# Moving one weight's pre-additions from the closing stage into the second half of a Winograd-form trunk kernel, regrouping the others, and deferring the gates' sigmoids

## The chip, the cores and the metric

The kernel runs on one core of one Trainium2 chip. The metric is device time in microseconds (us) of one execution. The engines go by these names: TensorE (PE, with PEld for its weight loads), VectorE (DVE), ScalarE (ACT), GpSimd (POOL), SyncE (SP), whose queue (SPq) issues nearly all DMAs.

## The reference, cut to what matters

The input x has 2048 rows of 1024 columns. All of it is fp32.

```python
shift, scale, gate = split(silu(c) @ w_ada + b_ada)
u = x * (1 + scale) + shift
q, k, v, a_gate, p_in, p_gate, m_a, m_p = split(u @ w_in)
a = (sliding_window_sink_attention(q, k, v, ...) * silu(a_gate)) @ w_attn_proj
p = ((multiscale_causal_pool(p_in) mixed per group) * pool_scale * silu(p_gate)) @ w_pool_proj
y = sigmoid(m_a) * a + sigmoid(m_p) * p
y = (y @ w_out) * (1 + gate)
out = layer_norm(alpha * x + y)
```

## The kernel before, in words

**The multiplications.** Every large product is done by the Winograd form of Strassen's scheme: the two operands are cut into 2x2 blocks, and seven block products replace eight. A `Quad` is one such multiplication for two output tiles. Its weight side is loaded into tiles `W` and `A` (lines 253 to 266). GpSimd makes the weight sums `sum1`, `mid` and `late` (lines 268 to 278), four of 128x512 per quad, two of them in `mid`. The other side is a *set*: seven tiles named B11, T1, T2, B21, T3, B22 and T4, of which the T's are sums of raw blocks (T1 = B12 - B11, T2 = B22 - T1, T4 = B21 - T2, T3 = B22 - B12; the code makes them in place). To keep fp32 accuracy each operand is split in a high part (a cast on ACT, line 306) and a low part (a subtraction on DVE, line 132), and one block product is three passes of four multiplications of 128x128 by 128x512. These twelve multiplications are called a product below; the code calls `tick` after each.

**The rings.** `ring` runs groups of two quads: ten products in `back`, four in `front`, so fourteen ticks for a group. `hooks[(group, tick)]` holds functions that are traced at that tick, and `defer(n, f)` traces `f` n ticks on. Instructions of `pe`, `act`, `dve`, `pool`, `sp` stay in the order in which they are traced; those of `nc.scalar` and so on may be moved by the scheduler. Each engine then executes its own instructions in that order, and an instruction that waits holds what is behind it.

**The stages.** A first half (its rings of gates, then attention), a second half (the same: its rings run from about 605 to 828 us, then attention to about 1178 us), and the closing stage ("mix"): a group that ends the second half, two groups of the attention projection and two of the pool projection for the first half of the rows, the same four for the second half, and four groups of w_out with the layer norm. The groups of the closing stage are numbered 0 to 12 here, with ticks counted through: group 1 is ticks 14 to 27. The set changes between two phases: its seven tiles are loaded and split in the last group of one phase and the first five ticks of the next (`planned`, `SPLIT_AT`), so from group 0 into 1, 2 into 3, 4 into 5, 6 into 7 and 8 into 9.

**The sums.** A set's raw blocks lie in DRAM, and before the set can be loaded its four T's must be there too. `sums_to` makes them for one of four slices: it loads two 128x1024 rooms (`spare`) by four DMAs of 256 KB, subtracts four times on POOL (128x512 each), and puts the four results by four DMAs of 256 KB. In the second half's rings it does so for the first half's `ain_d[0]` and `pin_d[0]`; for w_out it loads the weight, multiplies by 1 + gate on DVE and puts the four raw blocks, without sums. The closing stage then makes the sums of `ain_d[1]`, `pin_d[1]` and `wo_d`, one slice every eight ticks from tick 2 to tick 90 (line 1572). In the second half the starts are the tuple of line 1493, where 14 is the first tick of the second ring. `ph.spare()` takes rooms in turn from a cycle that includes the tiles of q, k and v until `ph.turns.clear()` is called, and four rooms of its own after that.

**The gates.** `gates_ahead` (line 599) loads the merge gates of a quad from DRAM and applies the sigmoid (line 607) right behind the load; the consumers are lines 618, 627 and 629 on DVE.

Of the kernel before, what the change touches and what calls it, by code (L numbers as in the profile page):

```python
# [14 lines left out]
AF = mybir.ActivationFunctionType  # L15
# [45 lines left out]
def kernel(  # L61
# [22 lines left out]
    nc = tc.nc  # L84
# [30 lines left out]
    def set_store(name):  # L115
        return {n: dp.tile([2, P, 2, CH], F32, name=f"{name}_{n}") for n in set_names}

    u1_d = set_store("u1")
    wo_d = set_store("wo")
    ain_d = [set_store(f"ain{s}") for s in range(2)]  # L120
    pin_d = [set_store(f"pin{s}") for s in range(2)]
# [3 lines left out]
    def cols(t, n):  # L125
        return t[:, n * CH : (n + 1) * CH]
# [69 lines left out]
    def put(q, store, name, i, src):  # L196
        q.dma_start(store[name][i // 2, :, i % 2, :], src)

    def sums_to(ph, store, i, load, work=None, sums=True):

        b = []

        def x(r, c):
            return b[r][:, c * CH : (c + 1) * CH]

        def fetch():
            b.extend((ph.spare(), ph.spare()))
            b.reverse()
            for r in (1, 0):
                load(b[r], r)  # L210

        def sub(out, a, c):
            return lambda: pool.tensor_tensor(x(*out), x(*a), x(*c), ALU.subtract)

        todo = [(0, fetch)]
        if work:
            todo += [(3, lambda: work(b[0], 0)), (3.5, lambda: work(b[1], 1))]
        made = [("B11", (0, 0)), ("B21", (1, 0)), ("B22", (1, 1))] if work else []
        if work and not sums:
            made.insert(1, ("B12", (0, 1)))  # L220
        puts = [(5 + 0.6 * n, *x) for n, x in enumerate(made)]
        if sums:
            at = 7.5 if work else 4
            for out, a, c, name in (
                ((0, 1), (0, 1), (0, 0), "T1"),
                ((1, 1), (1, 1), (0, 1), "T2"),
                ((1, 0), (1, 0), (1, 1), "T4"),
                ((0, 0), (1, 1), (0, 0), "T3"),
            ):
                todo.append((at, sub(out, a, c)))  # L230
                puts.append((at + 2.5, name, out))
                at += 1.5
        for at, name, z in puts:
            todo.append((at, lambda name=name, z=z: put(sp, store, name, i, x(*z))))
        return sorted(todo, key=lambda t: t[0])
# [9 lines left out]
    class Quad:  # L245
# [7 lines left out]
        def load(self, ph, own, q=nc.sync, e=nc.gpsimd):  # L253
            self.w, self.a22 = ph.weights(), ph.last(own)
            x = self.w
            if len(self.srcs[0].shape) == 3:
                for dst, src, half in ((x[:, 2, :], 1, 0), (self.a22, 1, 1), (x[:, 0, :], 0, 0), (x[:, 3, :], 0, 1)):
                    q.dma_start(dst.rearrange("p (k q) -> p k q", k=4), self.srcs[src][:, 4 * half : 4 * half + 4, :])
                if e is not None:
                    self.sum1(e)  # L260
                return
            q.dma_start(x[:, 2, :], self.srcs[1][:, 0:CH])
            q.dma_start(self.a22, self.srcs[1][:, CH:])
            q.dma_start(x[:, 0::3, :], by_two(self.srcs[0]))
            if e is not None:
                self.sum1(e)
# [187 lines left out]
    def defer(ticks, f):  # L454
        due.append((now[0] + ticks, len(due), f))
# [140 lines left out]
    def wide(ph, i):  # L596
        return ph.t.tile([P, D], F32, tag=f"wide{i}", bufs=1, name=f"wide{i}")

    def gates_ahead(name, s, m, raw):
        g = {}  # L600

        def ahead(ph, turn):
            for mi, t in (((0, 0), (1, 1)), ((0, 1), (1, 0)))[turn]:
                x = g[mi, t] = ph.c("g")
                sp.dma_start(x, gates_d[name][s, m + mi, t])
                if raw:
                    nc.scalar.activation(x, x, AF.Sigmoid)

        return g, ahead

# [854 lines left out]
    def second_phase(ph, opened, post, plan1):  # L1465
        groups, fills, _, turn = plan1
        cb = ph.t.tile([P, D], F32, tag="cb", bufs=1, name="cb")
        hooks = {}

        def gate_rows():  # L1470
            nc.scalar.dma_start(gate_d.rearrange("k p -> p k"), mod[:, 16:24], allow_slow_non_contiguous=True)
            nc.scalar.dma_start(cb, gate_d.rearrange("k p -> (k p)").partition_broadcast(P))

        def load_wo(x, k):
            for n in range(2):
                sp.dma_start(cols(x, n), wout[k, n])

        side = []
        for raw in (ain_d[0], pin_d[0]):
            for i in range(4):  # L1480
                side.append(sums_to(ph, raw, i, load_raw(raw, i)))
        for i in range(4):
            ks = (i, 4 + i)
            side.append(sums_to(
                ph,
                wo_d,
                i,
                lambda x, r, ks=ks: load_wo(x, ks[r]),
                lambda x, r: dve.tensor_tensor(x, x, cb, ALU.mult),
                False,  # L1490
            ))
        ahead, hooks = hooks, {}
        for start, todo in zip((14, 18.5, 23, 27.5, 32, 36.5, 41, 45.5, 57, 61, 65, 69), side):
            for offset, f in todo:
                at = int(start + offset) - 14
                hooks.setdefault((at // 14, at % 14), []).append(f)
        later_hooks, hooks = hooks, ahead
        hooks.setdefault((0, 2), []).append(gate_rows)
        planned(hooks, ph, u1_d, True)
        opened = ring(ph, [post], opened, hooks, groups[0], lambda tick: [front(ph, q, tick) for q in groups[0]])  # L1500
        hooks = later_hooks
        planned(hooks, ph, None, False)
        hooks.setdefault((3, 0), []).append(lambda: ph.turns.clear())
        turned(hooks, lambda i: turn(ph, i), 4)
        opened_by = [q for _, _, q in fills[:2]]
        return ring(ph, groups, opened, hooks, opened_by, lambda tick: [front(ph, opened_by[0], tick)])
# [54 lines left out]
    with Pools("mix", spare=4, p=2, c=8) as ph:  # L1561
        for k in range(4, KT):
            ta[k] = wide(ph, k)
        phases = [([plans[1][2]], None)]
        for s in range(2):
            phases.append((pairs(lambda m, s=s: attn_quad(s, m)), ain_d[s]))
            phases.append((pairs(lambda m, s=s: pool_quad(s, m)), pin_d[s]))
        outs = [out_quad(k) for k in range(0, S // P, 2)]
        phases.append(([outs[i : i + 2] for i in range(0, 8, 2)], wo_d))
        every = [(i, gi) for i, (groups, _) in enumerate(phases) for gi in range(len(groups))]  # L1570
        sides = [{} for _ in phases]
        for n, (raw, i) in enumerate((raw, i) for raw in (ain_d[1], pin_d[1], wo_d) for i in range(4)):
            for offset, f in sums_to(ph, raw, i, load_raw(raw, i)):
                at = int(2 + 8 * n + offset)
                i, gi = every[at // 14]
                sides[i].setdefault((gi, at % 14), []).append(f)
        for i, (groups, store) in enumerate(phases):
            hooks = sides[i]
            if i:
                planned(hooks, ph, store, False)  # L1580
            after, nxt = None, []
            if i + 1 < len(phases):
                planned(hooks, ph, phases[i + 1][1], True, groups=groups)
                nxt = phases[i + 1][0][0]
                after = lambda tick, nxt=nxt: [front(ph, q, tick) for q in nxt]
            else:
                for at, row in ((1, 2), (1, 3), (5, 4), (5, 5)):
                    hooks.setdefault((0, at), []).append(lambda row=row: load_z(ph, row))
            if i in (3, 5):
                ta.clear()  # L1590
            if i == 4:

                def vectors():
                    for name, src in (("gain", gain), ("lnb", lnb)):
                        vec[name] = wide(ph, len(vec))
                        sp.dma_start(vec[name], src.partition_broadcast(P))

                hooks.setdefault((-1, 5), []).append(vectors)
                hooks.setdefault((-1, 7), []).append(lambda: [load_z(ph, row) for row in range(2)])
            opened = ring(ph, groups, opened, hooks, nxt, after, i == 5)  # L1600
# [53 lines left out]
```

## Time and profile before

| what | value |
|---|---|
| median of 3 runs | 1692.15 us (1687.09 to 1692.64) |
| the profiled execution's own time | 1693.3 us |
| its span, first to last instruction | 1691.5 us |
| mean granted TensorE clock | 0.994 |
| PE busy | 1648.7 us, 97% of the span |
| DVE, ACT, POOL busy | 1193.7, 1030.0, 988.5 us |
| mean DMA rate | 199 GB/s |

The profile comes from one execution, whose own time is 1.8 us above its span and 1.15 us above the median of the runs. A row of the view by stretches gives, for a window in us from the start of the span, the busy time of each engine with its number of instructions, the granted clock, the share of the 16 DMA engines in use and the rate. A row of a timeline gives start, duration, engine, line, operation and tiles; brackets at its end hold the idle time before it and who ended that. A row of a group of instructions has the count, the busy time and the mean duration in ns, then the idle time before them.

### The profile page before, as it was taken

Reading aid. Unit: us, or ns where it says so; the run is one execution under the profiler, and the core shown is the slowest. Engines: PE = TensorE matmul, PEld = TensorE weight load, DVE = VectorE, ACT = ScalarE, POOL = GpSimd, SP = SyncE. Lnnn points to the kernel's source line nnn. Section 1 sums busy time; section 2 is a strip of 40 time slices with the busy share of each in tenths; the row PEclk is TensorE's granted clock in tenths of the full one; section 3 lists DMA queues with packets and bytes.
Section 4 is the critical chain, followed back from the end, with each engine's and each line's share of the span. In section 5 each row is a group of like instructions: output and inputs, shape, how many; then the busy total and the mean of one; then the engine's idle time right before and its main releaser. Section 6 shows DMA issues by size and latency. Waiting matters only on the chain.

```text
span 1691.5 us, 24675 instructions
## 1 busy us (share of the span) xinstructions
PE 1648.7 (97%) x8058; PEld 1384.4 (82%) x8058; DVE 1193.7 (71%) x2132; ACT 1030.0 (61%) x2150; POOL 988.5 (58%) x734
## 2 busy tenths in 40 slices
PE   7999999999999999999999999999999999999997
PEld 6788888888888888888788888888878777887886
DVE  6856545676857657357567677676669897989877
ACT  4755457878778755335578777876646445644452
POOL 3343437586857828762476867496567576533442
PEclk9999999999999999999999999999999999999999
DMA  9688843343432478766533344234979797888443
GB/s 359 219 279 307 197 161 102 101 132 108 149 107 99 135 248 308 267 231 211 190 114 99 114 130 156 81 114 135 336 247 363 262 360 259 318 283 271 150 150 112
DMA packets 188849, 336.79 MB, mean 199 GB/s; under 512 B 18336, under 2 KB 44080, under 8 KB 188720
## 3 DMA queue, kind: packets, MB, share of 16 engines
q1 hardware_dynamic: 185600, 330.96, 57.3%
q10 hardware_dynamic: 3088, 4.23, 1.0%
q8 instruction: 64, 1.05, 0.2%
q14 instruction: 65, 0.53, 0.1%
q0 software_dynamic: 32, 0.02, 0.0%
HBM read 227.96 MB, written 110.33 MB: 200 GB/s over the span
## 4 chain that ended last, share of the span: by engine, by line
PE 74%; DVE 8%; DMA 7%; ACT 4%; issue 3%; POOL 3%; SPq 1%; POOLq 0%; DVEq 0%; ACTq 0%
PE mm L57 48%; PE lg L57 19%; PE pv L57 4%; PE pt L57 4%; DVE w_set L132 1%; DMA ain_T<-spare 1%; ACT L L57 1%; DMA g<-ma_d 1%; DMA g<-mp_d 1%; DVE w_set L57 1%; DVE set_T L57 1%; POOL W L269 1%; DMA spare<-pin_B 1%; DVE L L57 1%; ACT w_set L57 1%
## 5 line engine op out<-in xcount | busy, mean ns | idle before, releaser
L57 PE MATMUL mm<-set_B,w_set 128*128 128x512 f32 x2664 | 655.8, 393 | 2.2 <-DVE w_set L132 1.2
L57 PEld LDWEIGHTS mm<-set_B,w_set 128*128 128x128 f32 x2664 | 497.1, 189 | 107.0 <-DVE w_set L132 2.4
L57 PE MATMUL mm<-set_T,w_set 128*128 128x512 f32 x1824 | 455.5, 396 | 5.9 <-DVE mm L57 3.9
L57 PE MATMUL lg<-set_T,w_set 128*128 128x512 f32 x1704 | 412.6, 392 | 10.5 <-DVE p L390 4.4
L57 PEld LDWEIGHTS mm<-set_T,w_set 128*128 128x128 f32 x1824 | 336.7, 189 | 76.2 <-DVE mm L57 6.5
L57 PEld LDWEIGHTS lg<-set_T,w_set 128*128 128x128 f32 x1704 | 319.9, 189 | 81.8 <-ACT w_set L306 5.2
L132 DVE TENSOR_TENSOR w_set<-W,w_set 128x1024 fp32r<-128x1024 f32 x137 | 197.8, 1445 | 142.3 <-ACT w_set L306 129.3
L306 ACT CAST w_set<-W 128x1024 fp32r<-128x1024 f32 x137 | 143.8, 1050 | 212.7 <-PE mm L57 124.3
L57 POOL TENSOR_TENSOR w_set<-W,w_set 128x512 fp32r<-128x512 f32 x120 | 157.3, 1318 | 116.9 <-ACT w_set L57 112.0
L269 POOL TENSOR_TENSOR W<-W,A 128x512 f32<-128x512 f32 x46 | 74.1, 1610 | 232.5 <-DMA A<-in_win_dram 63.5
L57 DVE TENSOR_TENSOR o<-pv,o 64x128 f32<-64x128 f32 x256 | 72.1, 282 | 133.7 <-ACT o L57 127.3
L57 POOL TENSOR_TENSOR spare<-spare 128x512 f32<-128x512 f32 x68 | 124.0, 1826 | 31.5 <-DMA spare<-pin_B 12.2
L57 POOL TENSOR_TENSOR W<-W 128x512 f32<-128x512 f32 x82 | 108.3, 1336 | 53.2 <-DVE sm L57 31.0
L57 ACT ACTIVATE L<-L,nm 128x257 f32<-128x257 f32 (+1 forms) x256 | 127.2, 499 | 9.3 <-DVE nm L57 3.7
L278 POOL TENSOR_TENSOR W<-W 128x512 f32<-128x512 f32 x46 | 72.8, 1583 | 95.9 <-DVE w_set L132 83.5
L57 DVE CUSTOM_DVE_ANT_0 L<-lg,bt,nsink 128x256 f32<-128x256 f32 (+1 forms) x256 | 111.7, 473 | 21.3 <-PE lg L57 11.9
L57 ACT CAST w_set<-W 128x512 fp32r<-128x512 f32 (+1 forms) x165 | 101.4, 628 | 20.9 <-POOL W L57 14.9
L273 POOL TENSOR_TENSOR W<-W 128x512 f32<-128x512 f32 x44 | 72.7, 1656 | 66.3 <-DVE w_set L132 57.2
L57 ACT COPY o<-pv 64x256 f32<-64x256 f32 x128 | 47.4, 370 | 75.9 <-PE pv L57 74.7
L57 DVE TENSOR_TENSOR ptl<-pt,pth 128x512 fp32r<-128x512 f32 (+1 forms) x128 | 85.7, 669 | 1.3 <-ACT pth L57 1.0
L274 POOL TENSOR_TENSOR W<-W 128x512 f32<-128x512 f32 x44 | 71.6, 1628 | 21.9 <-DMA W<-in_win_dram 18.9
L57 ACT ACTIVATE L<-L,sm 128x256 f32<-128x256 f32 (+1 forms) x128 | 64.3, 502 | 31.7 <-DVE sm L57 31.4
(230 smaller groups left out, 2398.2 us busy)
## 6 DMA issues: line engine op xcount, KB each, us to landing
W<-in_win_dram SPq DMA_DIRECT2D x42, 512.0 KB, 5.4
W<-in_win_dram SPq DMA_DIRECT2D x42, 256.0 KB, 3.7
A<-in_win_dram SPq DMA_DIRECT2D x42, 256.0 KB, 4.9
ag_d<-sig SPq DMA_DIRECT2D x32, 256.0 KB, 5.7
pg_d<-sig SPq DMA_DIRECT2D x32, 256.0 KB, 4.4
pg<-pg_d SPq DMA_DIRECT2D x32, 256.0 KB, 3.2
pin_B<-fin SPq DMA_DIRECT2D x32, 256.0 KB, 2.0
ag<-ag_d SPq DMA_DIRECT2D x32, 256.0 KB, 2.9
```

The lines of the kernel that those rows point to most:

```text
L57: return lambda *args, **kw: self.tc.keep_in_program_order(op(*args, **kw))
L132: engine.tensor_tensor(dst, src, as32(hi), ALU.subtract)
L269: e.tensor_tensor(self.w[:, 1, :], self.w[:, 2, :], self.a22, ALU.add)
L273: e.tensor_tensor(x[:, 1, :], x[:, 1, :], x[:, 0, :], ALU.subtract)
L274: e.tensor_tensor(x[:, 2, :], x[:, 0, :], x[:, 2, :], ALU.subtract)
L278: e.tensor_tensor(x[:, 3, :], x[:, 3, :], x[:, 1, :], ALU.subtract)
L306: a.copy(by_two(hi), raw)
```

## The change

It does three things. The four T sums of w_out are made in the second half's rings, right behind the scaling, so w_out's B12 isn't stored any more, and the closing stage makes no sums for w_out; the starts in the second half move together to make room, and `ph.turns.clear()` comes one group earlier. In the closing stage the remaining eight slices get starts written out by hand: 17, 20, 30, 42, 45, 59, 72 and 74. The sigmoid of a merge gate is traced one tick behind its load.

```diff
-    def sums_to(ph, store, i, load, work=None, sums=True):
+    def sums_to(ph, store, i, load, work=None):
...
         made = [("B11", (0, 0)), ("B21", (1, 0)), ("B22", (1, 1))] if work else []
-        if work and not sums:
-            made.insert(1, ("B12", (0, 1)))
         puts = [(5 + 0.6 * n, *x) for n, x in enumerate(made)]
-        if sums:
-            at = 7.5 if work else 4
-            for out, a, c, name in (
-                ((0, 1), (0, 1), (0, 0), "T1"),
-                ((1, 1), (1, 1), (0, 1), "T2"),
-                ((1, 0), (1, 0), (1, 1), "T4"),
-                ((0, 0), (1, 1), (0, 0), "T3"),
-            ):
-                todo.append((at, sub(out, a, c)))
-                puts.append((at + 2.5, name, out))
-                at += 1.5
+        at = 7.5 if work else 4
+        for out, a, c, name in (
+            ((0, 1), (0, 1), (0, 0), "T1"),
+            ((1, 1), (1, 1), (0, 1), "T2"),
+            ((1, 0), (1, 0), (1, 1), "T4"),
+            ((0, 0), (1, 1), (0, 0), "T3"),
+        ):
+            todo.append((at, sub(out, a, c)))
+            puts.append((at + 2.5, name, out))
+            at += 1.5
...
                 sp.dma_start(x, gates_d[name][s, m + mi, t])
                 if raw:
-                    nc.scalar.activation(x, x, AF.Sigmoid)
+                    defer(1, lambda x=x: nc.scalar.activation(x, x, AF.Sigmoid))
...
                 lambda x, r, ks=ks: load_wo(x, ks[r]),
                 lambda x, r: dve.tensor_tensor(x, x, cb, ALU.mult),
-                False,
             ))
         ahead, hooks = hooks, {}
-        for start, todo in zip((14, 18.5, 23, 27.5, 32, 36.5, 41, 45.5, 57, 61, 65, 69), side):
+        for start, todo in zip((14, 17.5, 21, 24.5, 28, 31.5, 35, 38.5, 43, 48.5, 58, 63.5), side):
...
-        hooks.setdefault((3, 0), []).append(lambda: ph.turns.clear())
+        hooks.setdefault((2, 0), []).append(lambda: ph.turns.clear())
...
-        for n, (raw, i) in enumerate((raw, i) for raw in (ain_d[1], pin_d[1], wo_d) for i in range(4)):
+        ain, pin = ain_d[1], pin_d[1]
+        for start, raw, i in (
+            (17, ain, 0), (20, ain, 1), (30, pin, 0), (42, ain, 2),
+            (45, ain, 3), (59, pin, 1), (72, pin, 2), (74, pin, 3),
+        ):
             for offset, f in sums_to(ph, raw, i, load_raw(raw, i)):
-                at = int(2 + 8 * n + offset)
+                at = int(start + offset)
```

## The prediction

> **What bounds the kernel now.** I read the page first, then the view by stretches over groups of fourteen products, then the timelines of PE, DVE and POOL around PE's waits. From the page and the chain of work that ended last:
>
> ```profile
> PE 1648.7 (97%) x8058; PEld 1384.4 (82%) x8058; DVE 1193.7 (71%) x2132; ACT 1030.0 (61%) x2150; POOL 988.5 (58%) x734
> 708.85 10.88 PE mm L57 x48
> ```
>
> PE is the bound nearly everywhere. Four products in a row take 10.88 us, so one takes 2.72 us and a group of fourteen 38.1 us. Time can be won only where a group takes longer. The second half's rings (first four rows, groups 0 to 3 of its second ring) and the closing stage's groups 1 to 8 (last eight rows) are:
>
> ```profile
> core 0: us, PE busy (x) PEld busy (x) DVE busy (x) ACT busy (x) POOL busy (x), PEclk, DMA share, GB/s
> 643.50:681.60 38.10, 38.10 (x170) 31.56 (x169) 22.90 (x17) 18.56 (x25) 31.44 (x19) 1.00 0.86 313
> 681.60:719.70 38.10, 38.10 (x170) 31.56 (x169) 15.04 (x12) 14.00 (x21) 29.66 (x21) 1.00 0.76 263
> 719.70:757.80 38.10, 38.10 (x170) 31.56 (x169) 22.43 (x20) 13.88 (x21) 25.73 (x18) 1.00 0.76 251
> 757.80:795.90 38.10, 38.10 (x170) 31.56 (x169) 30.29 (x33) 19.96 (x31) 9.49 (x7) 1.00 0.53 180
> ...
> 1217.90:1263.50 45.60, 41.37 (x170) 33.53 (x170) 33.40 (x27) 22.72 (x31) 29.60 (x18) 0.93 0.78 262
> 1263.50:1301.60 38.10, 38.10 (x170) 31.56 (x169) 34.87 (x29) 24.60 (x32) 25.92 (x14) 1.00 1.03 385
> 1301.60:1343.80 42.20, 39.96 (x170) 32.62 (x170) 37.80 (x34) 16.80 (x24) 30.47 (x17) 0.96 0.70 237
> 1343.80:1384.10 40.30, 38.64 (x170) 31.35 (x169) 37.83 (x35) 21.25 (x29) 22.29 (x12) 1.00 1.00 362
> 1384.10:1423.90 39.80, 38.94 (x169) 31.18 (x168) 32.41 (x28) 18.57 (x26) 27.60 (x15) 1.00 0.70 255
> 1423.90:1462.10 38.20, 38.20 (x169) 31.48 (x169) 30.39 (x28) 22.78 (x30) 27.40 (x17) 1.00 1.04 390
> 1462.10:1500.30 38.20, 38.20 (x168) 31.09 (x168) 35.80 (x36) 18.41 (x26) 17.11 (x10) 1.00 0.59 198
> 1500.30:1540.40 40.10, 38.62 (x171) 31.70 (x170) 37.04 (x37) 24.03 (x31) 11.00 (x8) 1.00 0.99 349
> ```
>
> Here is the whole prize. The second half loses nothing. In the closing stage group 1 loses 45.6 - 38.1 = 7.5 us, group 3 4.1, group 4 2.2, group 5 1.7, group 8 2.0, and groups 6 and 7 0.1 each: 17.7 us. No edit of this change can give more; the second half can only lose. The next rows, from PE's timeline, are the two largest waits:
>
> ```profile
> 1240.75 2.07 PE L57 MATMUL lg<-set_T,w_set 128*128 128x512 f32 x4 [4.00 <-DVE w_set L132]
> 1242.62 2.76 PE L57 MATMUL mm<-set_B,w_set 128*128 128x512 f32 x6
> ...
> 1328.30 4.48 PE L57 MATMUL lg<-set_T,w_set 128*128 128x512 f32 x12 [2.24 <-DVE p L390]
> ```
>
> Both end with DVE. Each costs more than itself: the granted clock of groups 1 and 3 is 0.93 and 0.96, and the six multiplications behind the first wait come at nearly half the usual rate. So 4.0 us of waiting became 7.5 us and 2.24 us became 4.1. [...] The rows decide: I take the doubled price for any wait from 2.2 us.
>
> Why was DVE late? Groups of its instructions in the 22.5 us that end with the first wait, its fastest w_set subtraction anywhere, and two pieces of POOL's timeline:
>
> ```profile
> L132 DVE TENSOR_TENSOR w_set<-W,w_set 128x1024 fp32r<-128x1024 f32 x4 | 8.1, 2034 | 3.5 <-ACT w_set L306 3.5
> L57 DVE TENSOR_TENSOR set_B<-set_B 128x1024 fp32r<-128x1024 f32 x2 | 4.0, 2018 | 0.0
> L368 DVE TENSOR_TENSOR mm<-lg,p 128x512 f32<-128x512 f32 x2 | 1.4, 685 | 0.0
> ...
> L132 DVE TENSOR_TENSOR w_set<-W,w_set x137: 1206/1226/2321, 62.2 to 1666.6; 128x1024 fp32r<-128x1024 f32 x137
> ...
> 1220.79 4.53 POOL L57 TENSOR_TENSOR spare<-spare 128x512 f32<-128x512 f32 x2
> 1227.50 4.52 POOL L57 TENSOR_TENSOR spare<-spare 128x512 f32<-128x512 f32 x2
> ```
>
> The same 128x1024 subtraction takes 1.21 us at best and 2.03 on average here, at most 2.32; the one that reads PSUM (L368) isn't stretched. So a POOL subtraction of a set sum that runs beside a DVE subtraction of SBUF operands costs DVE up to 2.32 - 1.21 = 1.1 us. Four ran in this window, up to 4.4 us, against a wait of 4.0. [...]
>
> **The change part by part.** *The closing stage's sums.* From the starts (subtractions at start + 4, 5.5, 7 and 8.5), subtractions by group 0 to 7 are 4, 8, 7, 7, 6, 8, 7, 1 before and 0, 7, 5, 8, 4, 8, 0, 0 after: 48 become 32. Prices, all over the closing stage's groups 0 to 8 for the first two rows, the second half's rings for the others:
>
> ```profile
> L57 POOL TENSOR_TENSOR spare<-spare 128x512 f32<-128x512 f32 x48 | 93.6, 1955 | 23.5 <-DMA spare<-pin_B 12.2 <-DMA spare<-ain_B 8.1 <-DMA spare<-wo_B 2.2
> L269 POOL TENSOR_TENSOR W<-W,A 128x512 f32<-128x512 f32 x18 | 28.0, 1553 | 68.3 <-DMA W<-y_d 15.7 <-DMA A<-in_wap_dram 14.4 <-DMA A<-in_wpp_dram 13.2
> ...
> L57 POOL TENSOR_TENSOR second_kk<-second_kk 128x512 f32<-128x512 f32 x8 | 12.9, 1618 | 0.2
> L57 POOL TENSOR_TENSOR spare<-spare 128x512 f32<-128x512 f32 x8 | 10.8, 1346 | 0.2
> ...
> spare<-wo_B SPq DMA_DIRECT2D x16, 256.0 KB, 5.1
> wo_T<-spare SPq DMA_DIRECT2D x16, 256.0 KB, 6.5
> wo_B<-spare SPq DMA_DIRECT2D x16, 256.0 KB, 5.2
> ```
>
> The closing stage loses 16 subtractions of 1.96 us, 16 loads and 16 stores of 256 KB, 8.4 MB. At the 385 GB/s of group 2 that is 22 us of transfer, taken from a stage whose groups 2, 4, 6 and 8 have a DMA share of 0.99 to 1.04. POOL and DMA are off PE's path there; only the waits count.
>
> Group 1: until tick 21 no subtraction is left, so DVE gets its 4.4 us back against a wait of 4.0, and groups 0 and 1 carry less traffic. The seven that remain run at ticks 21 to 28, where GpSimd must also make the next quads' sums; I leave 1 us, bounds 0 and 4. From 7.5 to 1: -6.5.
>
> Group 3: eight subtractions instead of seven, at ticks 46 to 53, where the two DVE operations per pool tile run; DVE was busy 37.8 of 42.2 us. Ticks 28 to 46 lose some four, worth up to 4.4 us of DVE, if that lead isn't lost in idling before tick 46. I take a remaining loss of 3 of 4.1, nearer to the present row than to none; bounds 0 and 6. -1.1.
>
> Group 4: four instead of six, 2.2 x 4 / 6 = 1.5, less a little for the lighter traffic, 1.2 (0 to 2.5). Group 5: eight before, eight after, later and closer together; 1.7 becomes 1.5 (0 to 4). Groups 6 and 7 lose nothing now and stay. Group 8 has no subtraction before or after; its 2.0 us stay but for the sigmoids.
>
> *The sigmoids.* ACT's own waits for the gates are
>
> ```profile
> L607 ACT ACTIVATE g<-g x64: 612/622/649, 1229.4 to 1513.9; 128x512 f32<-128x512 f32 x64
>   DMA g<-ma_d: 1.9, 2
>   DMA g<-mp_d: 0.6, 1
> ```
>
> 2.5 us of 64 sigmoids, and none of PE. Behind the waiting sigmoid ACT holds casts of sets and weights; in the new place they go first. Gain at most 2.5 us, spread over groups with slack. The other way, a sigmoid one product (2.72 us) later can hold line 618 or 627 on DVE and the casts of the next weights. I take -0.4, all in group 8 (2.0 to 1.6), bounds -1 and +2.
>
> *The second half.* It gets 16 subtractions on POOL, 16 T stores less four B12 stores, and the slices closer together. By the starts, its second ring's groups then hold 10, 16, 10, 7 and 5 subtractions. Group 1 now has 21 POOL instructions, of which eight belong to its quads, so 13 go to 16: 29.7 + 3 x 1.6 = 34.5 of 38.1 us. One more slice of 2 MB there brings 263 GB/s to about 315, what group 0 bears today (313) with PE at 38.10 of 38.10. Group 3 gets seven subtractions where it had none: at 1.1 us each DVE goes from 30.3 to at most 38.0 of 38.1. Of the scalings of w_out it had six (DVE's part of the rooms, same window):
>
> ```profile
> 757.80:795.90 38.10, 8.67 (x6) 0.00 (x0) 0.00 (x0) 1.00 0.53 180
> ```
>
> It keeps the four of two slices, so 8.67 / 3 = 2.9 us leave it: 35.1 us. That is the tight place. On SP, the loads of slices 10 and 11 come right behind the last stores from the rooms that they reuse (tick 58 behind 57, 63 behind 63); queued behind that wait are the weight loads of the next quads, and DVE's scaling waits in order for the load. SP's waits for such stores before, and the weight sum and cast with the least slack that I found:
>
> ```profile
> SPq L57 <- DMA wo_B<-spare: 10.4, 5, 5.5
> ...
> 702.02 1.30 POOL L269 TENSOR_TENSOR W<-W,A 128x512 f32<-128x512 f32 x1 [1.44 <-DMA W<-in_win_dram]
> ...
> 706.71 1.04 ACT L306 CAST w_set<-W 128x1024 fp32r<-128x1024 f32 x1
> ```
>
> The sum ends at 703.3, the product that needs it begins at 708.85 + 2 x 2.72 = 714.3; cast and low part take 1.0 and 1.2 to 2.3 us. So a load may come some 7.5 us late, and SP's longest wait for a store was 5.5. It is hidden in most cases; I take +0.5, bounds 0 and 5 (a wait of 2.5 us, doubled).
>
> **Sum.** -6.5 - 1.1 - 1.0 - 0.2 - 0.4 + 0.5 = -8.7 us. Against the profiled execution's own 1693.3 us: 1684.6. Its time is 1.15 us above the median, so against the median 1692.15 - 8.7 = 1683.4 us.
>
> **The rivals.**
>
> *All waits go.* If DVE is ahead everywhere, 17.7 us less 1.6 of group 8: 1676. For it: the traffic that is gone from the full groups. Against: groups 3, 4 and 5 keep eight, four and eight subtractions, with a DVE that was busy 32 to 38 us.
>
> *The gain stays in group 1 and is paid back in part* (no measurable change). Group 3's wait stays whole or grows, since its subtractions stand exactly where it waited (1328.3 is tick 51), groups 4 and 5 stay, and the second half loses 2: -6.5 + 1 + 2 = -3.5, 1688.6 us.
>
> *Slower: POOL becomes the bound where the sums are packed.* In groups 1, 3 and 5 seven or eight subtractions fall in about eight ticks, 21.8 us, together with the two `sum1` and four of `mid` that the next group's first products need. At the mean of 1.96 and 1.55 us that is 8 x 1.96 + 6 x 1.55 = 25.0 us. So POOL would end 3.2 us late; if a product waits for that and not for DVE, three waits of 3.2 us, doubled by the clock, make 19.2, and with 2.0 of group 8 and 2.2 of group 4 the loss is 23.4 against 17.7: 1697.9 us. It decides as soon as the delay exceeds the slack of the next weights' split. Against it: group 1 of the second half had 13 subtractions and waited for nothing; for it: DVE there is busy 15 us, here 33 and more.
>
> *The change doesn't do what it says:* the scheduler may put the deferred sigmoid where it was. That alters the sum by 0.4 us only and has no chance of its own.
>
> **How the numbers follow.** Forecast 0.54 (own range 1678 to 1688), all waits go 0.14, paid back 0.18, slower 0.14. A measurement of this kernel tells about 0.3% from no change, 5.1 us: under 1687.1 is faster, over 1697.2 slower. The first two cases and a little of the third are faster, less the forecast's upper edge: 0.68; no change 0.20; slower 0.12, the last case less its part under 1697.2. The range 1675 to 1695 takes in the first three cases and leaves out most of the last.
>
> **What would show it.** Right: group 1 of the closing stage takes 39 us or less, with clock 1.00; no POOL row of sums before tick 21; group 6 has no sums and a DMA share well under 1.04; the second half's groups stay at 38.1 us. Wrong: a PE wait in group 3 of the second half or at the attention's start (SP held by a store), or PE waits in groups 1, 3 and 5 ended by POOL's `sum1` or `mid`, or a group 1 that still loses 7 us, which would mean that the set loads and not the subtractions made DVE late.

## The result, and the profile after

The change takes 1695.64 us in the median (1692.04 to 1700.16) against 1691.40 for the kernel before on the same chip: a ratio of 1.0028, interval 1.0017 to 1.0040. It is slower by 0.28%, or 4.7 us, where 8.7 us of gain was forecast, and it lies just above the range. The profiled execution took 1694.27 us, its span 1692.4 us.

From the page of the changed kernel, the busy times, and from its view by stretches the second half's groups 2 and 3 of the second ring and the closing stage's groups 1 to 8 (columns as before: window, then the engines' busy times, granted clock, DMA share, rate):

```profile
PE 1647.5 (97%) x8058; PEld 1385.3 (82%) x8058; DVE 1189.3 (70%) x2132; ACT 1031.0 (61%) x2150; POOL 991.0 (59%) x734
...
718.60:756.70 38.10, 38.10 (x169) 31.55 (x169) 29.53 (x24) 12.83 (x20) 24.40 (x15) 1.00 0.69 235
756.70:796.90 40.20, 38.33 (x169) 31.43 (x168) 31.78 (x32) 20.64 (x31) 25.49 (x17) 1.00 0.67 223
...
1219.00:1257.00 38.00, 37.87 (x167) 31.04 (x166) 25.41 (x25) 18.63 (x26) 25.19 (x17) 1.00 0.66 233
1257.00:1297.00 40.00, 39.35 (x174) 32.26 (x173) 34.65 (x29) 24.69 (x32) 23.08 (x12) 1.00 0.91 329
1297.00:1336.30 39.30, 38.18 (x166) 30.74 (x165) 38.21 (x34) 17.19 (x24) 30.37 (x17) 1.00 0.80 287
1336.30:1384.00 47.70, 41.50 (x169) 33.51 (x168) 40.35 (x38) 24.09 (x31) 21.71 (x13) 0.93 0.92 336
1384.00:1422.20 38.20, 38.20 (x170) 31.65 (x169) 26.74 (x24) 17.75 (x25) 27.44 (x16) 1.00 0.63 216
1422.20:1460.30 38.10, 38.10 (x170) 31.56 (x169) 32.45 (x30) 25.51 (x35) 17.62 (x8) 1.00 0.99 362
1460.30:1498.40 38.10, 38.10 (x170) 31.56 (x169) 29.00 (x32) 15.31 (x20) 12.60 (x8) 1.00 0.39 123
1498.40:1541.10 42.70, 40.31 (x170) 32.54 (x169) 38.03 (x38) 23.50 (x31) 13.76 (x8) 0.96 1.01 358
```

The windows for groups 1 to 3 do not meet the first products exactly: by PE's timeline these groups begin at 1218.79, 1257.31 and 1296.33 us and group 4 at 1336.31, so they take 38.5, 39.0 and 40.0 us. Group 1 has lost nearly its whole excess: 45.6 us before, 38.5 now. Groups 3 and 5 take 2.2 and 1.6 us less. Against that, group 4 takes 47.7 us instead of 40.3, group 8 42.7 instead of 40.1, group 2 39.0 instead of 38.1, and the second half's group 3 40.2 instead of 38.1. The nine differences in these windows, those of groups 6 and 7 with them, sum to +1.7 us; the spans differ by 0.9. The profiled execution of the kernel before, at 1693.3 us, lies 1.9 us above the median of its runs, and that of the change 1.4 us below its own, so the two views show where time went but not the whole 4.7 us. The loss is not a failed gain in group 1. A new wait of about the same size stands three groups later. From PE's timeline of the changed kernel:

```profile
787.55 1.19 PE L57 MATMUL mm<-set_B,w_set 128*128 128x512 f32 x4 [1.87 <-DVE w_set L132]
...
1371.92 2.08 PE L57 MATMUL mm<-set_B,w_set 128*128 128x512 f32 x4 [5.71 <-DVE w_set L132]
...
1524.24 4.15 PE L57 MATMUL lg<-set_T,w_set 128*128 128x512 f32 x10 [2.26 <-DVE w_set L132]
```

All three end with a weight split on DVE, as before. They say who was late, not why. The reason appears on another engine, in the order of ACT's work. From ACT's timeline of the kernel before and of the changed kernel at the start of group 4, the latter with two rows of DVE's:

```profile
1344.30 2.14 ACT L57 CAST set_B<-set_B 128x1024 fp32r<-128x1024 f32 x2
...
1349.26 1.05 ACT L57 CAST set_T<-set_T 128x1024 fp32r<-128x1024 f32 x1
1350.21 2.19 ACT L607 ACTIVATE g<-g 128x512 f32<-128x512 f32 x4
```

```profile
1338.34 1.05 ACT L57 CAST set_B<-set_B 128x1024 fp32r<-128x1024 f32 x1 [1.15 <-DMA set_B<-ain_B]
...
1342.05 1.05 ACT L57 CAST set_T<-set_T 128x1024 fp32r<-128x1024 f32 x1
1343.67 2.59 ACT L604 ACTIVATE g<-g 128x512 f32<-128x512 f32 x4 [0.57 <-DMA g<-mp_d]
1346.16 1.03 ACT L57 CAST set_T<-set_T 128x1024 fp32r<-128x1024 f32 x1
...
1349.83 1.33 ACT L604 ACTIVATE g<-g 128x512 f32<-128x512 f32 x2 [0.64 <-DMA g<-mp_d]
1351.07 1.04 ACT L57 CAST set_B<-set_B 128x1024 fp32r<-128x1024 f32 x1
...
1352.14 1.23 DVE L57 TENSOR_TENSOR set_B<-set_B 128x1024 fp32r<-128x1024 f32 x1 [1.01 <-ACT set_B L57]
...
1370.18 1.69 DVE L132 TENSOR_TENSOR w_set<-W,w_set 128x1024 fp32r<-128x1024 f32 x1
```

The two halves of B11 are cast 12.7 us apart, with eight sigmoids between them, which wait twice for their gates (0.57 and 0.64 us), and the two casts of T1. DVE then idles 1.01 us for the second half and works without a gap until 1371.87, when the split that PE waits for is done. In the kernel before, B11's two casts stand together (`x2`) and no sigmoid between them.

Compare the two lists: the first four sigmoids stand right behind T1's first cast in both. The deferral did not move the sigmoids on ACT; it moved a cast behind them. This also shows that the order in which `act` keeps its instructions is looser than "as they are traced": T1's casts are traced at ticks 4 and 5, B11's second half at tick 3, and yet they run first.

The chain of work that ended last, followed back from this wait of PE, runs the same way (start, us, what):

```profile
1343.67 6.84 DMA g<-mp_d
...
1351.07 1.05 ACT set_B L57
1352.14 1.23 DVE set_B L57
...
1370.25 1.62 DVE w_set L132
```

It goes from a gate's load over the last sigmoid to B11's cast and then along DVE's list. No work of GpSimd is on it between 1336 and 1372 us.

### The profile page after: what moved, and what is told of

It reads as the page before. It is cut to its first block, busy times and chain, and to the rows that moved or that the text cites. A ratio compares the mean times of both kernels' runs of the same rounds, so it can differ in the third digit from the quotient of the medians.

```text
span 1692.4 us, 24649 instructions
## 1 busy us (share of the span) xinstructions
PE 1647.5 (97%) x8058; PEld 1385.3 (82%) x8058; DVE 1189.3 (70%) x2132; ACT 1031.0 (61%) x2150; POOL 991.0 (59%) x734
## 4 chain that ended last, share of the span: by engine, by line
PE 75%; DVE 9%; DMA 5%; ACT 4%; issue 3%; POOL 3%; SPq 1%; POOLq 0%; DVEq 0%; ACTq 0%
PE mm L57 48%; PE lg L57 19%; PE pv L57 4%; PE pt L57 3%; DVE w_set L132 1%; DVE set_T L57 1%; DMA g<-mp_d 1%; ACT L L57 1%; DVE w_set L57 1%; DVE g L624 1%; DMA W<-in_win_dram 1%; DVE wide L626 1%; ACT w_set L57 1%; DVE L L57 1%; SPq L57 1%
## 5 line engine op out<-in xcount | busy, mean ns | idle before, releaser
L57 POOL TENSOR_TENSOR W<-W 128x512 f32<-128x512 f32 x82 | 108.2, 1333 | 53.1 <-DVE sm L57 32.4
L57 POOL TENSOR_TENSOR spare<-spare 128x512 f32<-128x512 f32 x68 | 115.5, 1705 | 34.1 <-DMA spare<-pin_B 16.4
L275 POOL TENSOR_TENSOR W<-W 128x512 f32<-128x512 f32 x46 | 72.6, 1579 | 87.1 <-DVE w_set L132 69.7
L270 POOL TENSOR_TENSOR W<-W 128x512 f32<-128x512 f32 x44 | 79.9, 1820 | 64.2 <-DVE w_set L132 55.2
L271 POOL TENSOR_TENSOR W<-W 128x512 f32<-128x512 f32 x44 | 76.0, 1727 | 21.7 <-DMA W<-in_win_dram 15.2
```

Of the source, the lines that this page charges most:

```text
L57: return lambda *args, **kw: self.tc.keep_in_program_order(op(*args, **kw))
L270: e.tensor_tensor(x[:, 1, :], x[:, 1, :], x[:, 0, :], ALU.subtract)
L271: e.tensor_tensor(x[:, 2, :], x[:, 0, :], x[:, 2, :], ALU.subtract)
L275: e.tensor_tensor(x[:, 3, :], x[:, 3, :], x[:, 1, :], ALU.subtract)
```

## The experiments

Ratios below are to the kernel before, run in the same session; where two kernels are compared, so are their ratios. The first four take the change apart. Theory A was that the sums and their new places decide, theory B that the deferred sigmoids do.

**The change without the deferral.**

```diff
-                    defer(1, lambda x=x: nc.scalar.activation(x, x, AF.Sigmoid))
+                    nc.scalar.activation(x, x, AF.Sigmoid)
```

> The changed kernel with the sigmoid right behind its load again; everything else stays. Theory A (the sums decide: the subtractions on GpSimd stand in the wrong ticks of group 4, and those of w_out load group 3 of the second half): within 1.5 us of the changed kernel, so about 4 us above the kernel before, with the 5.9 us wait in group 4 and the 2 us wait in the second half still there. Theory B (the deferred sigmoids decide: they come late for the gates' consumers on DVE and re-order ACT): 3 us or more faster than the changed kernel, within 1.5 us of the kernel before or below it, and group 4's large wait gone.

Measured: 1687.97 us, ratio 0.9981 (0.9970 to 0.9992). One line moved the kernel from slower to faster, as theory B expected: 1.0028 against 0.9981 is 0.47% or 8 us. The wait of 5.71 us in group 4 is 1.61 here, and group 8's is 0.86. B11's two halves are cast back to back again. PE's row in group 4:

```profile
1370.17 1.20 PE L57 MATMUL mm<-set_B,w_set 128*128 128x512 f32 x4 [1.61 <-DVE w_set L132]
```

**The kernel before with the deferral alone.**

```diff
-                    nc.scalar.activation(x, x, AF.Sigmoid)
+                    defer(1, lambda x=x: nc.scalar.activation(x, x, AF.Sigmoid))
```

> The kernel before with the sigmoids one tick behind their loads, nothing else. Theory A: within 1.5 us of the kernel before. Theory B: 3 to 5 us slower, with a longer wait in a group of the pool projection (3, 4 or 8).

Measured: 1705.65 us, ratio 1.0083 (1.0066 to 1.0100), 14 us slower. Theory B has the sign right and the size far too small (3 to 5 us). Here PE waits for the set itself. Group 5, ACT's timeline of the kernel before, and then ACT's, DVE's and PE's of this one:

```profile
1389.59 2.00 ACT L57 CAST set_B<-set_B 128x1024 fp32r<-128x1024 f32 x2
...
1396.93 1.67 ACT L607 ACTIVATE g<-g 128x512 f32<-128x512 f32 x3
```

```profile
1391.10 1.05 ACT L57 CAST set_B<-set_B 128x1024 fp32r<-128x1024 f32 x1
...
1397.49 2.18 ACT L607 ACTIVATE g<-g 128x512 f32<-128x512 f32 x4
1399.58 1.03 ACT L57 CAST set_B<-set_B 128x1024 fp32r<-128x1024 f32 x1
...
1403.00 2.28 DVE L57 TENSOR_TENSOR set_B<-set_B 128x1024 fp32r<-128x1024 f32 x1
...
1400.66 1.20 PE L57 MATMUL mm<-set_B,w_set 128*128 128x512 f32 x4 [1.54 <-ACT set_B L57]
1405.34 3.77 PE L57 MATMUL mm<-set_B,w_set 128*128 128x512 f32 x8 [3.48 <-DVE set_B L57]
```

One half of B22 (`x1` and `x1` in place of `x2`) is cast behind four sigmoids. PE waits 1.54 us for this cast before the first multiplication of the product, makes four, and waits 3.48 us for the low part. The other half was cast at 1391.10 and yet no multiplication could begin, so the late one is the half that a product takes first. The cast, at 1399.58 us, did not pass the four sigmoids ahead of it, which began at 1397.49. Nor did the one in the changed kernel's group 4: the second half of B11 had landed by 1339.5 us (issued at 1333.0, landed within 6.5 us) and was cast at 1351.07, behind the last of the eight sigmoids.

**The change with regular starts, 2 + 8n.**

```diff
-        for start, raw, i in (
-            (17, ain, 0), (20, ain, 1), (30, pin, 0), (42, ain, 2),
-            (45, ain, 3), (59, pin, 1), (72, pin, 2), (74, pin, 3),
-        ):
+        for start, raw, i in [(2 + 8 * n, ain if n < 4 else pin, n % 4) for n in range(8)]:
```

> The changed kernel with the closing stage's eight slices every eight ticks from tick 2, as the kernel before has them; w_out's sums stay in the second half, sigmoids stay deferred. Theory A: group 1 gets its four subtractions back in ticks 14 to 18 and loses 4 to 7 us again; group 4's six subtractions lie earlier by one tick and spread wider, and its loss falls from 9.6 to about 3 us; the total within 3 us of the changed kernel. Theory B: group 4's loss stays near 9 us beside group 1's, so some 5 us slower than the changed kernel.

Measured: 1701.68 us, ratio 1.0063 (1.0047 to 1.0080). The hand-made starts are worth 0.35%, 6 us, with the deferral in place. That is theory B's time, but not its place: by PE's timeline group 4 takes 44.2 us, so its loss did not stay near 9.

**The change without the closing stage's subtractions.**

```diff
-            todo.append((at, sub(out, a, c)))
+            if subs:
+                todo.append((at, sub(out, a, c)))
...
-            for offset, f in sums_to(ph, raw, i, load_raw(raw, i)):
+            for offset, f in sums_to(ph, raw, i, load_raw(raw, i), subs=False):
```

> The changed kernel without the 32 subtractions of the closing stage's set sums; their loads and stores stay (the stored T blocks are then the raw ones). Theory A: the DVE subtractions of groups 1 to 5 lose their stretch, the waits of groups 1 to 5 together fall from about 13 us to under 4, and the kernel is 9 to 12 us faster than the changed one, 1683 to 1687 us. Theory B: the waits of groups 3, 4 and 8 remain, a gain of under 4 us.

Measured: 1687.60 us, ratio 0.9976 (0.9963 to 0.9988). The 32 subtractions still cost 0.52%, 8.8 us, about what theory A expected; waits of 2.59 us in group 4 and 1.99 in group 8 remain, as theory B expected. So both theories hold a price of the same size. Group 4's wait comes of the late cast and of subtractions that stretch DVE's work behind it: the last `set_T` low part ahead of the split takes DVE 2.29 us in the change (at 1365.69 us, with two of these subtractions on POOL until 1366.90 and a weight sum behind them) and 1.21 us here. But the kernel before makes 48 such subtractions in this stage, so the change takes some of A's price away; only B explains why it is slower.

The next runs ask how the deferral costs its 8 us, and what is left without it.

**The change with the set casts' order restored, deferral kept.** `SPLIT_AT` holds the ticks at which the fourteen halves of sets are cast, (2, 3, 4, 5, 6, 7, 11, 12, 13, 14, 15, 16, 17, 18) in both kernels. The new list casts B11's second half together with its first at tick 2, B22's first half at 14 instead of 15 (its second stays at 16), and both halves of T4 at 16; the text below speaks of B22's second half, but it is the first that moves. Ahead of the closing stage:

```diff
     ta, vec = {}, {}
+    SPLIT_AT = (2, 2, 4, 5, 6, 7, 11, 12, 13, 14, 14, 16, 16, 16)
```

> The change with its deferred sigmoids kept; only the list SPLIT_AT is another one in the closing stage, so that the second halves of B11, B22 and T4 are cast at the ticks of their first halves, ahead of the tick at whose end the deferred sigmoids are issued. Nothing is left out. In the program's order on ScalarE the second half of B11 then no longer stands behind all eight sigmoids, nor that of B22 behind four. Theory O (the deferral costs time because it puts set casts behind sigmoids that wait for their gate loads): the time falls by most of the 7.7 us that taking the deferral away gained, to 1686 to 1691 us, and the wait of 5.87 us in group 4 goes below 2.5. Theory L (the deferral costs time because the sigmoids themselves, and the multiplications by the gates, come later): it stays within 2 us of the change, 1694 to 1698 us, and group 4 keeps its wait.

Measured: 1687.57 us, ratio 0.9980 (0.9967 to 0.9992), the same as without the deferral. From its timelines of ACT, DVE and PE in group 4:

```profile
1343.69 1.05 ACT L57 CAST set_B<-set_B 128x1024 fp32r<-128x1024 f32 x1 [1.42 <-DMA set_B<-ain_B]
1344.98 1.05 ACT L57 CAST set_B<-set_B 128x1024 fp32r<-128x1024 f32 x1 [0.24 <-DMA set_B<-ain_B]
...
1344.77 2.52 DVE L57 TENSOR_TENSOR set_B<-set_B 128x1024 fp32r<-128x1024 f32 x2 [1.73 <-ACT set_B L57]
...
1372.68 1.20 PE L57 MATMUL mm<-set_B,w_set 128*128 128x512 f32 x4 [2.13 <-DVE w_set L132]
```

The low parts stand where DVE idled, the wait falls from 5.71 to 2.13 us, and the four multiplications behind it take 1.20 us instead of 2.08. Theory O (the order of the casts) is right, theory L (the sigmoids themselves come too late) wrong. The deferral itself gains nothing even so: 0.9980 with it, 0.9981 without.

**Two controls: this list without the deferral, and both on the kernel before.** The first is the change with the sigmoid behind its load and `SPLIT_AT` as above, the second the kernel before with the deferral and `SPLIT_AT` as above.

> A control for the kernel with restored cast order: the same list SPLIT_AT in the closing stage, but without the deferral (sigmoids right behind their loads). Theory O (the list gains only by taking the casts out from behind the deferred sigmoids): there is nothing to restore here, so the time is that of the change without the deferral, 1686.5 to 1689.5 us, ratio 0.997 to 0.999. Theory R (earlier casts are a gain of their own, and the deferral still costs its 8 us beside them): about 8 us less than with restored order and deferral, 1679 to 1682 us.

Measured: 1687.00 us, ratio 0.9975 (0.9963 to 0.9986). Theory O holds: the list adds nothing that can be told from the kernel without the deferral.

> The kernel before with the deferred sigmoid and the list SPLIT_AT of the closing stage that casts the second halves ahead of the deferred sigmoids. The deferral alone cost 14 us here, and PE waited directly for casts of set_B and their low parts, 1.30+1.40 us in group 1 and 1.54+3.48 us in group 5. Theory O: all of it is given back, 1689 to 1694 us, no wait of PE that ends with ACT or DVE set_B, and group 1's wait of 4 us for w_set is there again. Theory L (the sigmoids themselves come too late): 1700 us or more.

Measured: 1694.45 us, ratio 1.0018 (1.0005 to 1.0031), a little above what was expected. Of the 0.83% that the deferral cost, 0.65% are given back, and no wait of PE ends with set_B. The 4.03 us wait of group 1 is back. In its profile PE waits 0.66 and 0.52 us in group 7, where the kernel before has no such wait; whether that makes the remaining 0.18% stays open.

**Without the deferral: the subtractions, and the starts.** The same two edits as above.

> The change without the deferral, and without the 32 subtractions of the closing stage (loads and stores stay; the sets stored are then raw halves, not sums). Theory A (GpSimd's sums and the VectorE instructions that they stretch carry the closing stage's waits by themselves): the 8 us that the same cut gained with the deferral are gained here too, 1679 to 1682 us. Theory J (sums and deferral make the waits together, and either cut takes most of them): only the waits that the trace without the deferral still shows in groups 1, 3, 4 and 8 can go, 0.81+2.28+1.77+1.02 us and about 1.7 us of the half clock behind the second, 7.6 us at the most and half of it at the least, 1680.5 to 1684.5 us.

Measured: 1681.71 us, ratio 0.9942 (0.9924 to 0.9959), 0.39% or 6.6 us under the kernel without the deferral. The two theories' spans overlap at this value, so it doesn't choose between them. Its profile has no wait of PE left in groups 1, 3 and 4. It does show that the deferral costs about as much without these sums (0.9976 against 0.9942, 5.8 us) as with them (8 us); the difference is within the intervals.

> The change without the deferral, and with the eight slices of the closing stage at starts 2+8n in place of the hand-made ones: w_out's move to the second half alone. With the deferral these starts cost 6.0 us against the hand-made ones. Theory M (the move of w_out's sums alone makes the gain, and the hand-made starts were worth something only where the deferral had delayed the casts): within 1.5 us of the kernel without the deferral, 1686.5 to 1689.5 us. Theory S (the starts carry it: a regular slice in group 1 meets the change of sets): 1691 to 1695 us, with waits over 3 us in groups 1 to 3.

Measured: 1692.74 us, ratio 1.0011 (0.9997 to 1.0026). Theory S holds: the starts are worth 0.30%, 5 us, and a slice in group 1 brings the old wait back. So moving w_out's sums, by itself, gains nothing that can be told from zero; this kernel also has the longest wait in the second half, 3.11 us. PE's timeline in group 1:

```profile
1244.81 2.08 PE L57 MATMUL lg<-set_T,w_set 128*128 128x512 f32 x4 [4.03 <-DVE w_set L132]
```

**One scaling pair on GpSimd, and p_in's second slice earlier.**

```diff
-                lambda x, r: dve.tensor_tensor(x, x, cb, ALU.mult),
+                lambda x, r, e=pool if i == 2 else dve: e.tensor_tensor(x, x, cb, ALU.mult),
...
-            (45, ain, 3), (59, pin, 1), (72, pin, 2), (74, pin, 3),
+            (45, ain, 3), (56, pin, 1), (72, pin, 2), (74, pin, 3),
```

> The change without the deferral, with two corrections: the two scalings of w_out's third slice, which VectorE makes in the second half's keys-and-values group, are made by GpSimd, and p_in's second slice of the closing stage starts at tick 56 in place of 59, so that its four subtractions lie in the stretch where GpSimd sits idle for 17.8 us. Theory P (each remaining wait hangs on the VectorE work beside it): the 1.89 us wait of the second half and most of the 1.77+0.54 us of group 4 go, 1683 to 1686 us. Theory Q (the slack goes to another place: GpSimd is the slower engine for a scaling and stretches VectorE beside it): no change or a loss, 1687 to 1691 us, and a wait stays in the second half's group 3.

Measured: 1687.97 us, ratio 0.9983 (0.9970 to 0.9996), no gain. Theory Q holds, though the second half's wait stands one group later than it said; the run changes two things, and what each costs can't be told apart. Timelines of POOL, DVE and PE:

```profile
779.80 5.75 POOL L57 TENSOR_TENSOR spare<-spare,cb 128x1024 f32<-128x1024 f32 x2 [5.73 <-DMA spare<-in_wout_dram]
...
793.07 3.46 DVE L57 TENSOR_TENSOR spare<-spare,cb 128x1024 f32<-128x1024 f32 x2 [5.02 <-DMA spare<-in_wout_dram]
...
798.79 2.07 PE L57 MATMUL lg<-set_T,w_set 128*128 128x512 f32 x4 [2.32 <-DVE w_set L132]
...
1372.35 2.08 PE L57 MATMUL mm<-set_B,w_set 128*128 128x512 f32 x4 [3.24 <-DVE w_set L132]
```

GpSimd took 5.75 us for the two scalings that took DVE 2.36 in the kernel without the deferral. The second half's wait only moved to 10 us later, behind the next slice's load, and group 4's grew from 1.61 to 3.24 us.

**The second half's wait: the subtractions or the place.** The first kernel leaves w_out's 16 subtractions out, the second starts w_out's last two slices later; both have no deferral.

```diff
-            todo.append((at, sub(out, a, c)))
+            if store is not wo_d:
+                todo.append((at, sub(out, a, c)))
```

> The change without the deferral, and without the 16 subtractions that make w_out's sums in the second half; its loads, scalings and stores keep their places (the four T sets of w_out are then raw halves). Theory C (the 1.9 us wait of the second half's keys-and-values group comes from the subtractions themselves, which stretch VectorE's instructions beside them): the wait goes, 1684.5 to 1686.5 us. Theory D (it comes from where the scalings stand: the sums hold the four rooms longer, so that the third slice's load lands late and VectorE starts both scalings of it behind a wait): the rooms are held as long as with the subtractions, the wait stays at 1.5 us or more, and the time is 1687 to 1689 us.

```diff
-        for start, todo in zip((14, 17.5, 21, 24.5, 28, 31.5, 35, 38.5, 43, 48.5, 58, 63.5), side):
+        for start, todo in zip((14, 17.5, 21, 24.5, 28, 31.5, 35, 38.5, 43, 48.5, 61, 66), side):
```

> The change without the deferral, and with w_out's third and fourth slices of the second half started at ticks 61 and 66 in place of 58 and 63.5, 8.2 and 6.8 us later. Theory C: the subtractions of the second slice still run beside the keys-and-values group, the wait stays within 1 us of 1.9, and the time within 1.5 us of the kernel without the deferral, 1686.5 to 1689.5 us. Theory D: VectorE no longer waits for the load of the third slice inside that group, the wait falls below 0.6 us and the time to 1685 to 1687 us.

Measured: 1686.05 us, ratio 0.9967 (0.9954 to 0.9980), and 1683.98 us, ratio 0.9962 (0.9948 to 0.9976). The later starts make the fastest complete kernel of this study by its ratio, 0.38% under the kernel before (the interval overlaps that of the cast list without the deferral). Either edit takes the wait away (1.73 us without the deferral, 0.28 without the subtractions, none with the later starts), so it needs both causes: theory C's forecast holds for the first kernel, theory D's for the second, which came out 1 us below its range. First PE's row without the subtractions; then SP's and DVE's timelines of the kernel without the deferral, and the same of the one with later starts:

```profile
786.60 1.20 PE L57 MATMUL mm<-set_B,w_set 128*128 128x512 f32 x4 [0.28 <-DVE w_set L132]
```

```profile
772.15 0.60 SPq L57 DMA_DIRECT2D wo_T<-spare  x1
772.80 2.97 SPq L57 DMA_DIRECT2D spare<-in_wout_dram  x4
...
780.58 2.36 DVE L57 TENSOR_TENSOR spare<-spare,cb 128x1024 f32<-128x1024 f32 x2 [1.59 <-DMA spare<-in_wout_dram]
```

```profile
765.47 0.42 SPq L57 DMA_DIRECT2D wo_T<-spare  x1
765.99 2.27 SPq L57 DMA_DIRECT2D spare<-in_wout_dram  x4
...
774.40 1.22 DVE L57 TENSOR_TENSOR spare<-spare,cb 128x1024 f32<-128x1024 f32 x1
```

Requested three ticks later, the load runs 6.8 us earlier: at tick 58 the order built for SP puts it behind a store of the slice before (772.15), at tick 61 ahead of that store. So `sp` doesn't keep strictly to the ticks either. The scaling then finds its data at 774.40 and DVE no longer waits for the load inside the dense part of the group.

## Why the prediction was wrong, point by point

**The sigmoids: the step that failed.** The prediction gave them -0.4 us, bounds -1 and +2, from 2.5 us of idle time that ACT spends on gate loads. It had the direction of the queue backwards: "behind the waiting sigmoid ACT holds casts of sets and weights; in the new place they go first". In the built order B11's casts had already gone first, and the deferral put the second half of B11 behind eight sigmoids and one half of B22 behind four, while the first sigmoids kept their place. Measured: +8 us on the change, +14 us on the kernel before, and given back by the casts' order alone. The prediction read ACT's idle time before the sigmoids, 2.5 us, as the thing at stake. It wasn't: with the change it even rose, to 5.4 us, while the price lay in what was queued behind:

```profile
  DMA g<-mp_d: 4.3, 5
  DMA g<-ma_d: 1.1, 3
```

In the kernel before with the deferral alone the same two rows are 0.6 and 0.2 us, with the largest loss of all. The bound on the bad side named line 618 and the casts of the next weights, not the sets, although the order of set casts and sigmoids stood in ACT's timeline.

**Group 1: right.** Forecast 45.6 to about 39, measured 38.5 with clock 1.00. Without the deferral it takes 39.0, and the regular starts then bring the wait of 4.03 us back. The first sum in this group starts at 1235.67 us instead of 1220.79.

**Groups 3 and 5: right sign here, not for the reason given.** -1.1 and -0.2 forecast, -2.2 and -1.6 in the profile. But without the deferral, with the same sums at the same places, group 3 takes 42.1 us, as before, after a wait of 2.12 us behind which eleven multiplications take 4.32 us. So the regrouping alone gained nothing in group 3, and its gain in the change is luck as far as the prediction goes.

**Group 4: wrong.** -1.0 forecast, +7.4 measured, with a granted clock of 0.50 behind the wait (1371.92 to 1374.00 us; 2.08 us for four multiplications, 1.20 without the deferral). Without the deferral the group takes 40.3 us, as before: all of the +7.4 belongs to the failed step, and the forecast gain isn't there either. Counted from the group's first product, the split that PE waits for starts 4.3 us later than with the restored order. Of this, 2.3 us are there when DVE makes T1's second low part, the next set work behind B11's; the other 2.0 come after that, where DVE's list has one more pair of gate instructions (`wide`, 1.75 us, and `g`, 0.68) ahead of the split and one small split less.

**Group 8: wrong, same step.** -0.4 forecast, +2.6 measured; 0.86 us of wait without the deferral against 2.26 with it. The same pattern stands here: B11's halves are cast at 1499.03 and 1512.24 us with eight sigmoids between them, and the chain of work that ended last passes through that second cast.

**The second half: mechanism named, size missed.** The tight place was named (group 3, DVE at 35.1 of 38.1 us, scalings behind a load that waits for a store's room). +0.5 was taken, +2.1 measured, inside the bounds 0 to 5. DVE was not as full there as forecast (31.8 us busy, not 35.1); the scalings stood in its list behind a late load, ahead of the split that PE needed. The wait was said to be hidden in most cases; it stood in every kernel with these starts, these subtractions and the scalings on DVE (0.96 to 3.11 us).

**The sum.** Without the sigmoid term it came to -8.3 us; the same kernel measured 0.9981, -3.2 us. So a second part of the prediction was mis-sized as well. By that kernel's profile group 1 kept most of its gain, groups 3 and 4 took 42.1 and 40.3 us, as before, instead of 1.1 and 1.0 less, and the second half's group 3 took 40.1 instead of 38.1. With the second half's starts mended the kernel measured 0.9962, -6.4 us.

**The rivals.** The one on the other side, GpSimd as the bound, gave 1697.9 us. Its number is near the measured one, but its mechanism did not occur: no wait of PE in these groups ends with `sum1` or `mid`, and the chain behind the new wait passes over no GpSimd work. "Paid back in part" (1688.6 us: group 3's wait stays, groups 4 and 5 stay, the second half loses 2) is nearly what the change without the deferral did, at 1687.97 us. For the sums this rival was the better forecast, and it had 0.18 against 0.54.

**What would show it.** Group 6 without sums: right; no sum before tick 21: right to within a tick. Group 6's DMA share "well under 1.04": 0.99, hardly. The second half's groups at 38.1 us: wrong in group 3, the place named for it.

## What to carry to other kernels

Moving an instruction that waits for a DMA a step later in the source can move other work behind it, as it did here with B11's second cast, 12.7 us after the first: read the built order on its engine, and ask which casts that PE needs stand behind it, whatever its own idle time was. Here the deferral cost nothing only when the casts were traced ahead of the sigmoids, and it gained nothing then. When a change joins several edits, a run without each of them tells which one has the price: one line held 8 us here. A load requested later can run earlier, if it thereby leaves its place behind another slice's store; here it was issued at 765.99 us instead of 772.80.

## What the runs showed of the hardware

In these runs the length of a wait does not decide how fast the multiplications behind it come. From PE's timelines of the change with regular starts, of the kernel with later w_out starts, and of the one with regular starts and no deferral:

```profile
1329.46 4.53 PE L57 MATMUL lg<-set_T,w_set 128*128 128x512 f32 x12 [1.78 <-ACT w_set L303]
```

```profile
1320.07 3.01 PE L57 MATMUL lg<-set_T,w_set 128*128 128x512 f32 x12 [2.04 <-DVE p L387]
```

```profile
790.96 1.20 PE L57 MATMUL mm<-set_B,w_set 128*128 128x512 f32 x4 [3.11 <-DVE w_set L132]
```

After 1.78 us of waiting twelve multiplications took 4.53 us; after 2.04 us they took 3.01, and after 3.11 us four took 1.20. In the changed kernel four took 1.19 us after 1.87 us of waiting, at a granted clock of 1.00 (787.55 to 788.70 us), and 2.08 after 5.71 us, at 0.50. The prediction's rule, a doubled price for any wait from 2.2 us, is too simple on both sides. No run here places waits on purpose, so what decides the rate behind a wait is not shown.
